# Decoder layer on one core: the first weight piece and the first part of x loaded as two halves each, the first products ordered block by block, new issue orders

## The chip, the cores and the metric

One core of a Trainium2 chip runs the whole kernel. TensorE (PE) multiplies, with its weight loads shown apart (PEld); VectorE (DVE), ScalarE (ACT) and GpSimd (POOL) work elementwise; SyncE (SP) issues most of the loads. The metric is the device time of one execution, in microseconds (us).

## What is computed

One layer of a decoder over 256 positions of 1024 channels, in float32: a normalised x times a wide input matrix, two attention mixers on parts of the product, two gates, an output projection with a residual, and an MLP.

```python
h = _rmsnorm(x, norm1_g[i])
proj = h @ w_in[i]                      # 1024 x 6308, split into q, k, v, gates
y_a = _nsa_mixer(q_a, k_c, v_c, k_s, v_s, k_w, v_w, g_nsa, ...)
y_b = _dilated_mixer(q_b, k_b, v_b)
mixed = sigmoid(g_ma) * (y_a @ w_o_a[i]) + sigmoid(g_mb) * (y_b @ w_o_b[i])
x = x + mixed @ w_out[i]
h2 = _rmsnorm(x, norm2_g[i])
x = x + square(relu(h2 @ w_up[i])) @ w_down[i]
```

## The kernel before

**Products in three parts.** Every float32 operand is split into a rounded high part and the rest: `wh` and `wl` of a weight piece, `hT[0]` and `hT[1]` of the scaled x. A product is the sum of `wh`·`hT[0]`, `wh`·`hT[1]` and `wl`·`hT[0]`. So a weight piece (128 partitions x 768 numbers, 384 KB; those of kv_w 840 numbers) takes three steps before PE can use all of it: its load into `raw`, ACT's rounding into `wh` (line 345; for the very first piece two casts on DVE, line 349), and DVE's subtraction into `wl` (line 350). A piece of an input projection then gives PE 12 matmuls (two row blocks `kk` of the piece, two halves `t` of the positions, three parts).

**The head.** x comes in four parts `xg[0..3]` of two blocks of 128 channels each; `xg[0]` begins with the 16 gains. `scale_x(k)` makes block k of `hT[0]` on ACT (line 415) and of `hT[1]` on DVE (line 416). `setup()` squares the four parts on ACT (`sx`, line 426), adds them on POOL (line 428), sums over partitions on PE (line 432), and gets the reciprocal root `rs` from DVE (`ss`, line 435) and POOL (line 436); POOL also makes the tables `ropeg` from `rope` and `gr` (lines 444 and 447). Before all that PE multiplies the tile `ones` by itself ten times (line 408). The first projections are the chunks kv_c (compressed keys and values, line 468), kv_s and kv_w (lines 479 to 481), then q_a and so on, with attention in between; the last stage is the MLP.

**What sets the order.** `ORDER` is a table of numbers for each engine: the instructions in the order in which the code writes them, renumbered into the order in which they are to be issued (`issue_order`). An engine issues strictly in that order, so an instruction that waits holds everything behind it on its engine; loads on SP and ACT hold the queue in the same way. Eight semaphores (DMAHW0 to DMAHW7 in the rows below) serve all loads in turn: a load that reuses one waits until its last user has landed.

**Buffers.** `once` gives a tile a place of its own. The tile `y` collects the attention outputs, `x1` holds x for the residual (line 1116) and the later sums.

Of the kernel before, what the change touches and what calls it, by code (L numbers as in the profile page):

```python
# [11 lines left out]
F32 = mybir.dt.float32  # L12
# [11 lines left out]
NT = 2  # L24
# [96 lines left out]
1 0 2 4 3 9+2 104 15 13 12 16 11 19 14 20 18 5 17 6 8 7 21+83 105+60 166 165 167+4 172 171 173+5 179 178  # L121
180+4 185 184 186+4 191 190 192+5 198 197 199+2""",
    "ACT": """
# [15 lines left out]
474 473 475+3 479 478 481 480 482 484 483 485+3 489 488 491 490 492 494 493 495+3 499 498 501 500 502+38""",  # L139
    "DVE": """  # L140
# [20 lines left out]
635+2 634 637+4 643 641 644 642 645+4 650+2 649 652+2""",  # L161
    "PE": """
# [83 lines left out]
def hybrid_layer(ctx: ExitStack, tc: tile.TileContext, A, out):  # L246
# [60 lines left out]
    def load_to(end):  # L307
        while len(raws) < min(end, len(pieces)):
# [4 lines left out]
            if q < 4:  # L313
                nc.sync.dma_start(xg[q], A["xg"][:, q * 512 + 16 * (q > 0):(q + 1) * 512 + 16])
# [972 lines left out]
```

## Time and profile before

| | |
|---|---|
| median of 3 runs | 459.05 us (459.05 to 459.7) |
| the profiled execution: time | 458.8 us |
| its span, first to last instruction | 457.0 us (1.8 us lie around it) |
| first product of the layer on PE | 11.12 us |
| mean granted TensorE clock | 0.993 of full speed |
| PE, PEld, DVE, ACT, POOL busy | 445.6, 431.1, 358.0, 284.2, 83.7 us |

Busy time is an average over stages with different limits: the head up to about 30 us, the attention stage up to about 260 us, and the rest. A row of the trace gives a start, a duration, the engine, the line, output<-inputs and shapes, and, where the engine stood idle before it, in brackets how long and what ended that.

### The profile page before, as it was taken

To read this page: it belongs to the slowest core of one execution; us is meant where nothing else is said; L and a number is where in the kernel's file an instruction comes from. 1 tells how busy PE (TensorE), PEld (TensorE's weight loads), DVE (VectorE), ACT (ScalarE), POOL (GpSimd) and SP (SyncE) were. 2 spreads that over 40 slices of the span, in tenths; PEclk is the share of its full clock that TensorE was granted. 3 is DMA by queue.
4 is the path that set the end of the run, shared out by engine and by line. 5 is a ranking of instruction groups with operands and counts; after the bars stand their busy time and mean duration, and the time that the engine had idled before them with its cause. 6 is when DMAs were issued, how large, how long until landed. Compare 5 with 4: busy or idle time off the path is not lost.

```text
span 457.0 us, 9071 instructions
## 1 busy us (share of the span) xinstructions
PE 445.6 (98%) x3413; PEld 431.1 (94%) x3413; DVE 358.0 (78%) x654; ACT 284.2 (62%) x622; POOL 83.7 (18%) x92
## 2 busy tenths in 40 slices
PE   4999999999999999999999999999999999999996
PEld 4999899899999999898999999999999999999996
DVE  3989999999999998899999886886856654555440
ACT  4855677678999778876775555665665634433330
POOL 2712121313041000200000001796322300000000
PEclk9799999999999999999999999999999999999999
DMA  8974586725535522541521647666666667677620
GB/s 304 367 244 146 154 287 181 236 89 167 157 105 141 171 70 71 175 140 68 162 82 42 199 128 231 201 193 186 205 184 195 183 187 210 185 216 199 179 78 13
DMA packets 29484, 76.92 MB, mean 168 GB/s; under 512 B 3664, under 2 KB 5120, under 8 KB 29312
## 3 DMA queue, kind: packets, MB, share of 16 engines
q1 hardware_dynamic: 28864, 74.77, 54.7%
q10 hardware_dynamic: 576, 1.57, 1.0%
q8 instruction: 27, 0.44, 0.4%
q14 instruction: 17, 0.14, 0.1%
HBM read 75.28 MB, written 1.05 MB: 167 GB/s over the span
## 4 chain that ended last, share of the span: by engine, by line
PE 93%; DVE 2%; ACT 2%; DMA 2%; issue 0%; ACTq 0%
PE acc L983 19%; PE acc L985 19%; PE acc L984 19%; PE acc L480 6%; PE acc L481 6%; PE acc L479 6%; PE tp L709 3%; PE acc L468 2%; DMA raw<-in_kv_c 2%; PE sp L754 1%; PE pvo L721 1%; ACT wh L345 1%; PE pvo L723 1%; PE tp L552 1%; PE dsp L920 1%; PE hacc L615 1%
## 5 line engine op out<-in xcount | busy, mean ns | idle before, releaser
L350 DVE TENSOR_TENSOR wl<-raw,wh 128x768 fp32r<-128x768 f32 (+2 forms) x183 | 177.6, 979 | 61.7 <-ACT wh L345 57.2
L345 ACT CAST wh<-raw 128x768 fp32r<-128x768 f32 (+1 forms) x182 | 149.6, 833 | 102.1 <-PE acc L984 74.5
L983 PE MATMUL acc<-u,wh 128*128 128x256 f32 x256 | 71.6, 280 | 0.0
L984 PE MATMUL acc<-u,wh 128*128 128x256 f32 x256 | 71.6, 280 | 0.0
L985 PE MATMUL acc<-u,wl 128*128 128x256 f32 x256 | 71.5, 279 | 0.0
L984 PE MATMUL acc<-h,wh 128*128 128x256 f32 x256 | 69.0, 280 | 0.0
L983 PE MATMUL acc<-h,wh 128*128 128x256 f32 x256 | 69.0, 279 | 0.0
L985 PE MATMUL acc<-h,wl 128*128 128x256 f32 x256 | 66.1, 279 | 0.0
L480 PE MATMUL acc<-wl,hT 128*128 128x384 f32 (+1 forms) x164 | 55.1, 350 | 0.3 <-DVE wl L350 0.3
L479 PE MATMUL acc<-wh,hT 128*128 128x384 f32 (+1 forms) x164 | 54.7, 348 | 0.0
L481 PE MATMUL acc<-wh,hT 128*128 128x384 f32 (+1 forms) x164 | 54.6, 347 | 0.0
L1159 POOL TENSOR_TENSOR r<-r 128x256 f32<-128x256 f32 x32 | 27.7, 866 | 128.7 <-ACT r L1158 127.5
L985 PEld LDWEIGHTS acc<-u,wl 128*128 128x128 f32 x256 | 48.2, 188 | 0.0
L983 PEld LDWEIGHTS acc<-u,wh 128*128 128x128 f32 x256 | 48.1, 188 | 0.0
L984 PEld LDWEIGHTS acc<-u,wh 128*128 128x128 f32 x256 | 48.1, 188 | 0.0
L983 PEld LDWEIGHTS acc<-h,wh 128*128 128x128 f32 x256 | 47.6, 188 | 0.0
L984 PEld LDWEIGHTS acc<-h,wh 128*128 128x128 f32 x256 | 47.4, 188 | 0.0
L985 PEld LDWEIGHTS acc<-h,wl 128*128 128x128 f32 x256 | 45.8, 188 | 0.0
L502 POOL TENSOR_TENSOR st<-st,nhalf 128x6 f32<-128x6 f32 (+1 forms) x16 | 21.6, 1348 | 92.8 <-DVE st L501 65.7
L984 PE MATMUL acc<-hT,wh 128*128 128x256 f32 x128 | 36.1, 293 | 0.0
L985 PE MATMUL acc<-hT,wl 128*128 128x256 f32 x128 | 35.9, 293 | 0.0
L983 PE MATMUL acc<-hT,wh 128*128 128x256 f32 x128 | 35.1, 290 | 0.0
(212 smaller groups left out, 986.9 us busy)
## 6 DMA issues: line engine op xcount, KB each, us to landing
raw<-in_cells SPq DMA_DIRECT2D x128, 384.0 KB, 3.4
raw<-in_cw SPq DMA_DIRECT2D x10, 384.0 KB, 3.2
raw<-in_q_a SPq DMA_DIRECT2D x8, 384.0 KB, 3.8
raw<-in_q_b SPq DMA_DIRECT2D x8, 384.0 KB, 3.4
raw<-in_k_b SPq DMA_DIRECT2D x8, 384.0 KB, 3.2
raw<-in_v_b SPq DMA_DIRECT2D x8, 384.0 KB, 3.1
raw<-in_kv_w SPq DMA_DIRECT2D x4, 420.0 KB, 6.7
raw<-in_kv_c ACTq DMA_DIRECT2D x4, 384.0 KB, 7.0
```

Source lines behind the costliest of these rows:

```text
L345: nc.scalar.copy(hi[:, :m], src)
L350: nc.vector.tensor_sub(lo[:, :m], src, f(hi[:, :m]))
L468: nc.tensor.matmul(acc[t][:, :n], hT[h][:, k, t * 128:(t + 1) * 128], w[:, kk * n:(kk + 1) * n], start=h == 0 and k == 0 and w is hi, stop ...
L479: nc.tensor.matmul(o, hT[0][:, k, ts], hi[:, c], start=k == 0, stop=False)
L480: nc.tensor.matmul(o, hT[0][:, k, ts], lo[:, c], start=False, stop=False)
L481: nc.tensor.matmul(o, hT[1][:, k, ts], hi[:, c], start=False, stop=k == 7)
L502: nc.gpsimd.tensor_tensor(st[:, 1, :h], st[:, 0, :h], nhalf[:, :h], op=OP.pow)
L709: nc.tensor.transpose(pt[0:rows, i * 128:(i + 1) * 128], s, ident)
L983: nc.tensor.matmul(o, hi, a[0][k], start=start, stop=False)
L984: nc.tensor.matmul(o, hi, a[1][k], start=False, stop=False)
L985: nc.tensor.matmul(o, lo, a[0][k], start=False, stop=stop)
L1159: mul = nc.gpsimd.tensor_mul(r, r, r)
```

## The change

The first piece of kv_c is loaded as two halves of 384 columns (192 KB each), and `xg[0]` as 272 and 256 columns (136 and 128 KB), each half with a semaphore of its own. The matmuls of the first three pieces are written block by block. `y` and `x1` now ask for one shared place by a common tag. All five tables of `ORDER` are new; of these the diff shows a line each.

```diff
     "SP": """
-1 0 2 4 3 9+2 104 15 13 12 16 11 19 14 20 18 5 17 6 8 7 21+83 105+60 166 165 167+4 172 171 173+5 179 178
+0+4 12 10 14 4 17 20 16 5 21 13 9 15 11 18+2 6+3 22+80 105 102+3 106+60 167 166 168+4 173 172 174+5 180 179
...
     "ACT": """
-0+4 6 10 13 9 4+2 7+2 11 16 15 14 17 12 19+2 25+4 18 21 47 22 24 35 48 36 23 49 38 41 37 58 42 29+2 32+2 43
+0+7 10 9 8 11 7 16+2 12 14+2 26 20+2 13 27+2 18 29 25 24 19 22+2 33 36 48 34 37 30+2 39 49+2 59 32 55 51+3
...
             raw = raw_p.tile([128, n], F32, name="raw", tag="raw" if n <= PIECE else "rawg")
+            if q == 0:
+
+                nc.sync.dma_start(xg[0][:, 0:272], A["xg"][:, 0:272])
+                nc.scalar.dma_start(raw[:, 0:n // 2], src[:, 0:n // 2])
+                nc.sync.dma_start(xg[0][:, 272:528], A["xg"][:, 272:528])
+                nc.scalar.dma_start(raw[:, n // 2:n], src[:, n // 2:n])
+                raws.append(raw)
+                continue
             if q < 4:
-                nc.sync.dma_start(xg[q], A["xg"][:, q * 512 + 16 * (q > 0):(q + 1) * 512 + 16])
+                nc.sync.dma_start(xg[q], A["xg"][:, q * 512 + 16:(q + 1) * 512 + 16])
...
-                for h, w in ((0, hi), (1, hi), (0, lo)):
-                    for kk in range(2):
-                        k = i * 2 + kk
-                        for t in range(NT):
...
+                for h, w, kk in [(0, hi, 0), (0, hi, 1), (1, hi, 0), (1, hi, 1), (0, lo, 0), (0, lo, 1)]:
+                    k = i * 2 + kk
+                    for t in range(NT):
...
-    st_["y"] = once([128, 8, S], F32, "y")
+    st_["y"] = big.pool.tile([128, 8, S], F32, name="y", tag="y", bufs=1)
...
-    x1 = big.tile([128, 8, S], F32, name="x1", tag="y", bufs=1)
+    x1 = big.pool.tile([128, 8, S], F32, name="x1", tag="y", bufs=1)
```

The start of ACT's queue before: the four loads of kv_c, the load of the function table, and then two roundings of weight pieces (`wh`) and two squarings (`sx`) ahead of the first block of `hT`.

```order
L315 DMA raw_80<-in_kv_c 128x768
L315 DMA raw_83<-in_kv_c 128x768
L315 DMA raw_86<-in_kv_c 128x768
L315 DMA raw_89<-in_kv_c 128x768
L345 ACT_TABLE_LOAD
L345 CAST wh_160<-raw_83 128x768 [waits DMAHW3_49]
L426 ACTIVATE sx1_181<-xg1_77 128x512 [waits DMAHW1_49]
L345 CAST wh_215<-raw_86 128x768 [waits DMAHW5_49]
L426 ACTIVATE sx0_180<-xg0_76 128x512 [waits DMAHW2_49]
L415 ACTIVATE hT0_137<-xg0_76 128x256 x2
```

The same place after the change.

```order
L308 DMA raw_80<-in_kv_c 128x384
L310 DMA raw_80<-in_kv_c 128x384
L315 DMA raw_85<-in_kv_c 128x768
L315 DMA raw_88<-in_kv_c 128x768
L315 DMA raw_91<-in_kv_c 128x768 [waits DMAHW1_49]
L415 ACT_TABLE_LOAD
L415 ACTIVATE hT0_139<-xg0_76 128x256
L415 ACTIVATE hT0_139<-xg0_76 128x256 [waits DMAHW2_49]
L426 ACTIVATE sx0_182<-xg0_76 128x512
L415 ACTIVATE hT0_139<-xg1_77,xg0_76 128x256 [waits DMAHW4_49]
L415 ACTIVATE hT0_139<-xg1_77,xg0_76 128x256
L426 ACTIVATE sx1_183<-xg1_77 128x512
```

`hT` moved to the front, and each block waits for its own part of x. There are five loads now, and the fifth reuses the semaphore of the first half of `xg[0]` (DMAHW1), so the table load and all behind it stand behind that landing.

The start of DVE's queue before: the two casts of the first piece, three subtractions (`wl`), then `hT[1]`.

```order
L349 CAST wh_155<-raw_80 128x384 [waits DMAHW0_49]
L349 CAST wh_155<-raw_80 128x384
L350 TENSOR_TENSOR wl_156<-raw_80,wh_155 128x768 [waits DVE_49]
L350 TENSOR_TENSOR wl_161<-raw_83,wh_160 128x768 [waits DMAHW3_49,Activation_49]
L350 TENSOR_TENSOR wl_216<-raw_86,wh_215 128x768 [waits DMAHW5_49,Activation_49]
L416 SCALAR_TENSOR_TENSOR hT1_138<-xg0_76,hT0_137 128x256 [waits DMAHW2_49,Activation_49]
```

The same place after the change.

```order
L416 SCALAR_TENSOR_TENSOR hT1_140<-xg0_76,hT0_139 128x256 [waits DMAHW1_49,Activation_49]
L349 CAST wh_157<-raw_80 128x384 [waits DMAHW0_49]
L416 SCALAR_TENSOR_TENSOR hT1_140<-xg0_76,hT0_139 128x256 [waits DMAHW2_49,Activation_49]
L349 CAST wh_157<-raw_80 128x384 [waits DMAHW3_49]
L350 TENSOR_TENSOR wl_158<-raw_80,wh_157 128x768 [waits DVE_49]
L416 SCALAR_TENSOR_TENSOR hT1_140<-xg1_77,xg0_76,hT0_139 128x256 [waits DMAHW4_49,Activation_49]
```

The two blocks of `hT[1]` now stand ahead of the two casts, so DVE's first instruction waits for ACT's first block of `hT[0]`, and the first cast stands behind it.

ACT's queue before, about 20 us later, at the first reading of `rs` (POOL makes `rs`; `vSW` and `y` are products times `rs`; `wh_243`, `wh_265` and `wh_269` are the second to fourth piece of kv_s).

```order
L345 CAST wh_326<-raw_273 128x840 [waits DMAHW3_49]
L345 CAST wh_243<-raw_94 128x768 [waits DMAHW5_49,DVE_49,PE_49]
L345 CAST wh_265<-raw_96 128x768 [waits DMAHW7_49,DVE_49,PE_49]
L562 ACTIVATE vSW_295<-acc_462,rs_140 128x3x64 [waits PE_49,Pool_49]
L345 CAST wh_269<-raw_98 128x768 [waits DMAHW1_49]
L573 ACTIVATE y_291<-acc_150,rs_140 128x384 [waits DVE_49,PE_49,Activation_49]
```

The same place after the change; those three pieces are now `wh_245`, `wh_267` and `wh_271`.

```order
L345 CAST wh_328<-raw_275 128x840 [waits DMAHW1_49,DVE_49]
L572 ACTIVATE y_293<-acc_152,rs_142 128x384 [waits PE_49,Pool_49]
L572 ACTIVATE y_285<-acc_151,rs_142 128x384 [waits PE_49]
L345 CAST wh_245<-raw_96 128x768 [waits DMAHW0_49]
L345 CAST wh_267<-raw_98 128x768 [waits DMAHW1_49]
L345 CAST wh_271<-raw_100 128x768 [waits DMAHW2_49,DVE_49]
```

The two `y`, which wait for `rs` (Pool_49), moved ahead of all three of these pieces.

On SP the load of `gr` moves from the 7th to the 17th place and waits for the second piece of kv_w; the load of `x1` moves from the 8th to the 103rd place, into the attention stage. On POOL `rs` moves ahead of four of the six tables, behind the two first ones, and the tile `ones` is set before `vC` and one of the two `pc`.

## Rows read from the trace of the kernel before

**Rows 1.** Two windows: busy us (instructions) of PE, PEld, DVE, ACT, POOL; clock; DMA.

```profile
12.00:260.00 248.00, 247.02 (x1747) 233.04 (x1746) 235.63 (x495) 182.62 (x455) 37.31 (x33) 0.99 0.51 155
260.00:457.00 197.00, 193.14 (x1648) 192.88 (x1646) 118.03 (x154) 96.24 (x160) 43.11 (x47) 1.00 0.61 176
```

**Rows 2.** PE's longest wait of the span: total us, times, longest.

```profile
PE acc L468 <- ACT hT L415: 4.1, 1, 4.1
```

**Rows 3.** Timeline of PE: the warm-up, the first product, two spacings, the 38th product.

```profile
2.45 4.58 PE L408 MATMUL acc<-ones 128*128 128x128 f32 x20 [2.45 <-POOL ones L403]
11.12 3.13 PE L468 MATMUL acc<-wh,hT 128*128 128x384 f32 x8 [4.09 <-ACT hT L415]
...
15.01 0.52 PE L468 MATMUL acc<-wh,hT 128*128 128x384 f32 x1
15.33 0.52 PE L468 MATMUL acc<-wl,hT 128*128 128x384 f32 x1
...
17.53 0.51 PE L468 MATMUL acc<-wh,hT 128*128 128x384 f32 x2
17.88 0.51 PE L468 MATMUL acc<-wl,hT 128*128 128x384 f32 x2
...
22.04 0.42 PE L468 MATMUL acc<-wh,hT 128*128 128x384 f32 x1
```

**Rows 4.** Windows of the head: columns as in rows 1; the last are clock, DMA share, GB/s.

```profile
0.00:5.00 5.00, 2.55 (x12) 2.56 (x13) 0.00 (x0) 1.28 (x1) 1.86 (x11) 1.00 0.62 185
10.00:11.00 1.00, 0.00 (x0) 0.00 (x0) 0.83 (x1) 1.00 (x4) 0.26 (x1) 0.63 1.06 417
11.00:12.00 1.00, 0.88 (x3) 0.89 (x4) 1.00 (x2) 1.00 (x4) 1.00 (x1) 0.50 1.04 398
17.00:18.00 1.00, 1.00 (x7) 1.00 (x6) 1.00 (x2) 0.15 (x1) 0.17 (x1) 0.96 1.09 403
```

**Rows 5.** Timeline of ACT and its queue in the head.

```profile
0.72 2.10 ACTq L315 DMA_DIRECT2D raw<-in_kv_c  x4
2.85 1.28 ACT L345 ACT_TABLE_LOAD   x1 [2.85 <-issue]
10.57 0.89 ACT L415 ACTIVATE hT<-xg 128x256 fp32r<-128x256 f32 x2
```

**Rows 6.** Timeline of DVE in the head.

```profile
5.01 0.63 DVE L349 CAST wh<-raw 128x384 fp32r<-128x384 f32 x2 [5.01 <-DMA raw<-in_kv_c]
8.39 0.96 DVE L350 TENSOR_TENSOR wl<-raw,wh 128x768 fp32r<-128x768 f32 x1 [1.75 <-ACT wh L345]
10.16 0.96 DVE L350 TENSOR_TENSOR wl<-raw,wh 128x768 fp32r<-128x768 f32 x1 [0.82 <-ACT wh L345]
11.10 1.84 DVE L416 SCALAR_TENSOR_TENSOR hT<-xg,hT 128x256 fp32r<-128x256 f32 x2
15.55 0.47 DVE L416 SCALAR_TENSOR_TENSOR hT<-xg,xg,hT 128x256 fp32r<-128x256 f32 x1
23.70 3.10 DVE L350 TENSOR_TENSOR wl<-raw,wh 128x840 fp32r<-128x840 f32 x3
29.87 1.93 DVE L350 TENSOR_TENSOR wl<-raw,wh 128x768 fp32r<-128x768 f32 x2 [1.23 <-PE acc L480]
```

**Rows 7.** Timeline of POOL in the head.

```profile
10.74 1.52 POOL L428 TENSOR_TENSOR sx<-sx,sx 128x512 f32<-128x512 f32 x1 [3.58 <-ACT sx L426]
18.44 5.24 POOL L444 TENSOR_TENSOR ropeg<-rope,gr 128x256 f32<-128x256 f32 x5 [1.26 <-DMA rope<-in_rope]
23.63 0.72 POOL L436 TENSOR_TENSOR rs<-ss,nhalf 128x2 f32<-128x2 f32 x1
```

**Rows 8.** DMA issues: KB each, median us from issue to landing.

```profile
x<-in_xg SPq DMA_DIRECT2D x1, 1024.0 KB, 8.9
gr<-in_gr SPq DMA_DIRECT2D x1, 384.0 KB, 6.9
```

**Rows 9.** DVE's longest wait for PE from 10 to 260 us: total us, times, longest.

```profile
DVE nm L791 <- PE sp L756: 2.1, 5, 0.6
```

More of the change, by code (lines that the diff above doesn't have):

```diff
@@ L120 @@
     "SP": """
-1 0 2 4 3 9+2 104 15 13 12 16 11 19 14 20 18 5 17 6 8 7 21+83 105+60 166 165 167+4 172 171 173+5 179 178
-180+4 185 184 186+4 191 190 192+5 198 197 199+2""",
+0+4 12 10 14 4 17 20 16 5 21 13 9 15 11 18+2 6+3 22+80 105 102+3 106+60 167 166 168+4 173 172 174+5 180 179
+181+4 186 185 187+4 192 191 193+5 199 198 200+2""",
     "ACT": """
[15 rows of a table removed]
-474 473 475+3 479 478 481 480 482 484 483 485+3 489 488 491 490 492 494 493 495+3 499 498 501 500 502+38""",
-    "DVE": """
[20 rows of a table removed]
-635+2 634 637+4 643 641 644 642 645+4 650+2 649 652+2""",
-    "PE": """
[60 rows of a table removed]
-2575+17 2597 2592+3 2598 2595 2599+20 2620 2619 2621+767""",
[15 rows of a table added]
+474 476+3 480 479 482 481 483 485 484 486+3 490 489 492 491 493 495 494 496+3 500 499 502 501 503+38""",
+    "DVE": """
[20 rows of a table added]
+649 652+2""",
+    "PE": """
[52 rows of a table added]
+2139+2 2163+2 2129+10 2141+6 2188+2 2147+16 2212+2 2165+18 2187 2183+4 2190+22 2214+1174""",
     "POOL": """
-28 25 2 15 14 0+2 7 3+3 11+2 10 9 8 6 13 18 17 16 19+3 23+2 22 26+2 34+2 38 37 40 29 39 30 33 31 36 32 42 41
-45+5 44 50+5 56 55 57+4 62 61 63+11 43 74+14""",
+0 28 15 14 1+2 25 7 3+3 13 11 6 12 8 10 9 18+2 16+2 20+2 23 22 24 26+2 34+2 38+2 29 37 30 40 33 36 31+2 42
+41 45+3 43 50 48+2 51+2 44 53+2 56 55 57 59 58 60+28""",
 }
@@ L462, in proj @@
             if first and i < D["hh"]:
-                for h, w in ((0, hi), (1, hi), (0, lo)):
-                    for kk in range(2):
-                        k = i * 2 + kk
-                        for t in range(NT):
-                            nc.tensor.matmul(acc[t][:, :n], hT[h][:, k, t * 128:(t + 1) * 128],
-                                             w[:, kk * n:(kk + 1) * n], start=h == 0 and k == 0 and w is hi, stop=False)
+                for h, w, kk in [(0, hi, 0), (0, hi, 1), (1, hi, 0), (1, hi, 1), (0, lo, 0), (0, lo, 1)]:
+                    k = i * 2 + kk
+                    for t in range(NT):
+                        nc.tensor.matmul(acc[t][:, :n], hT[h][:, k, t * 128:(t + 1) * 128],
+                                         w[:, kk * n:(kk + 1) * n], start=h == 0 and k == 0 and w is hi, stop=False)
                 pe(12 * n / 2400)
```

180 rows, old and new, of the table ORDER are left out of this document.

## The prediction, made before the changed kernel ran

> **What bounds the kernel now.** I read the windows first, stage by stage. From 260 us to the end DVE works 118 of 197 us, while PE and its weight loads fill 193 [rows 1]: the last 197 us are PE's alone, the change leaves their work as it is, and whatever happens earlier shifts them. From 12 to 260 us both are nearly full: PE shows 247 of 248 us, but its weight loads only 233; DVE is busy 235.6, so it pauses 12.4 us in all [rows 1]. In this stretch neither can be moved far without the other. DVE makes every `wl`, and PE can't finish a weight piece without it.
>
> PE's waits come next: one is far longer than all others, 4.1 us for ACT's first `hT` [rows 2]. The timeline of the head shows why. The warm-up multiplications run from 2.45 to 7.03, and the first product starts at 11.12 [rows 3]. `hT` began on ACT at 10.57 [rows 5], although the first weight piece had landed at 5.01 [rows 6]. ACT was given other work first. The pause has a second price: the granted clock falls in the slice from 10 to 11 (0.63 in the mean, so at about 10.3), stays at 0.50, the lower of the two levels (1.2 GHz), and is back at 17 to 18 [rows 4]. In that stretch two products start 0.32 us apart, afterwards two take 0.35 together, 0.175 each [rows 3]. By 22.04 PE has started its 38th product of the layer [rows 3].
>
> **Head: when can the first product start?** In the first 5 us the DMA moves 185 GB/s x 5 us = 925 KB [rows 4], and the first piece of 384 KB lands at their end, since the other loads move beside it. The two first halves are 192 + 136 = 328 KB. The trace has no landing of such a half. Upper bound: no earlier than the whole piece, 5.0. Lower bound: the same end with only the missing half piece taken off at the 400 GB/s that the DMA reaches once it is full [rows 4], twice because two queues share it: 2 x 192 / 400 = 1.0, so 4.0. I take 4.2, nearer the lower end, because both queues now hold half as much ahead of it.
>
> ACT then has a wait that it did not have: the fifth load of its queue waits for the half of `xg[0]`, and the table load of 1.28 us stands behind it; before, it ran at 2.85 while nothing was there to work on [rows 5]. So: landing 4.2, one issue 0.4 (four took 2.10, so 0.5 at most), table load 1.28, makes 5.9; first block of `hT[0]` 0.45 (two took 0.89), 6.35. DVE's first block of `hT[1]`, which now stands ahead of the cast, 0.47 when POOL is idle [rows 6], 6.8; the cast 0.31, 7.1; with three hand-overs of about 0.1 each (10.57 + 0.45 to 11.12 is 0.1) **the first product starts at 7.4**, 3.7 earlier. From the bounds it is 7.2 to 8.7, the upper with 0.5 for the issue and 0.92 for `hT[1]` as at 11.10 [rows 6].
>
> The table load is where the Trainium skill and the trace differ. "ScalarE: Activation LUTs", section "What ACT_TABLE_LOAD costs", counts about 2.66 us for a load with its drain. By that figure the first product would start 1.4 later, at 8.8, and the sum below would lose as much; the 1.28 of [rows 5] is used.
>
> **Clock.** `ones` is set earlier (one `pc` and `vC` go behind it), so the warm-up ends by about 6.2, my estimate from the sum of those two fills, 0.8. The pause before the first product is then about 1.2 us instead of 4.1, and before the change the clock still stood at full for about 3.3 us after the last warm-up (7.03 to 10.3). So I expect 1.00 all through the head. That returns half of the 5.9 us from 11.12 to 17.0, 2.95.
>
> **PE by the 38th product.** 38 x 0.175 = 6.65 from 7.4 makes 14.05; waits for `hT[1]` and `wl`, which DVE delivers one by one (0.92 a block beside POOL's additions of 1.52 each [rows 6, 7]), I put at 1.3: three pieces, each with about 0.4. So 15.3 instead of 22.0: **PE gains 6.7**.
>
> **DVE by about 30 us.** Its work up to there is the same instructions in another order. It begins at 6.4 instead of 5.01: -1.4. Its three pauses (1.75 and 0.82 for ACT, 1.23 for PE [rows 6]) go: +3.8. Against that stands a new wait: after the ninth `wl` DVE needs the second kv_s piece, `wh_245`, which on ACT stands behind both `y`, which need `rs`. By my walk DVE gets to `ss` at about 21.5; `gr`, now the 17th load, is issued at about 13.9 (behind the landing of the second kv_w piece, issued near 7) and lands 6.9 later at most [rows 8], 20.8; two tables of 1.05 each (5.24 / 5) and `rs` 0.72 [rows 7] make 22 to 23.6; two `y` and a rounding add 1.5. DVE's three `wl` at this place began at 23.70 before, the third at about 25.4 [rows 6]; `wl_246` would begin between 23.5 and 25. The wait costs 0 to 2.4. Part of it is free, because POOL's tables slow DVE only when DVE works. I take 0.4: **DVE gains 2.0** (0 to 2.4).
>
> **The sum.** From 30 to 260 us the gain lies between DVE's 2.0 and PE's 6.7. DVE is the fuller engine, so I start from 2.0. Of its remaining 11.2 us of pauses (12.4 less the 1.23) some are waits for PE, 2.1 in the largest group [rows 9], and these shrink with PE ahead; I put that at 1.3. The sum is 3.3.
>
> The other edits are put at nothing. The load of `x1`, 1024 KB, leaves the head, where it took 8.9 us to land and about 2.5 us of a full DMA [rows 4, 8]; that helps the later weight pieces, and is part of their being in time above. At its new place, late in the attention stage, the DMA is half idle (0.51 busy from 12 to 260 [rows 1]); if it came too late for the residual, each us would be lost whole. The block order moves matmuls without adding any. The new order of the attention stage I can't price from the trace; its bounds are DVE's 11.2 us of pauses as a gain and the same again as a loss, and I see no reason for a sign, so it stands in the range.
>
> 458.8 - 3.3 = 455.5 for an execution like the profiled one. That one lies 0.25 under the median of 459.05, so the predicted time is **455.7 us**.
>
> **Rivals.** *PE's gain carries through*: DVE's pauses later are mostly waits for products, and its lead in buffered pieces lets it give way. Time: 459.05 - 6.7 = 452.3. For it: DVE waits for PE at 28.6 with all buffers full [rows 6]. Against it: 95% busy.
>
> *The halves land no earlier.* The Trainium skill's "DMA: Bandwidth & Descriptors", section "Bandwidth", asks for loads batched to 1 MiB or more, which speaks against cutting 384 KB in two. As a mechanism here: both halves land at 5.0, as the whole did; the first product starts at 8.2, and the gain shrinks by 0.8 to 2.5, 456.5. Against it: with 925 KB moved by 5.0, the wait was mostly for other loads' bytes.
>
> *No change*: the head's gain is spent where DVE is full; the wait for `rs` costs its whole 2.4, and the new attention order adds DVE pauses of about 2. Time: 459.
>
> *Slower*: `gr` lands late. In the head SP's loads stood in line for up to 8.9 us [rows 8], and now ropeg, `rs`, both `y`, three kv_s pieces and all that DVE splits from them stand behind this one load. Each us after 20.8 delays DVE by one; from 25 (20.8 + 3.3 + the 0.9 by which `ss` is later than needed) it is slower than before. A landing at 27 gives 461. Against it: `x1` has left that line.
>
> **Chances and range.** Forecast 0.47, PE's gain whole 0.2, halves no earlier 0.1, no change 0.13, slower 0.1. A change under 0.2%, 0.9 us, can't be told from none in this kernel. Faster: 0.47 + 0.2 + 0.1, with 0.01 from the fourth case: 0.78; same 0.11; slower 0.11. The range for 8 in 10 reaches from a little beyond the second case, 451.5, to the fourth, 459.2; the forecast's own is 453.5 to 457.5.
>
> **What would show it.** First product at 7.2 to 8.7; the table load right before the first `hT`, at about 4.6 instead of 2.85; clock 1.00 in every slice of the head; the 38th product near 15.3; DVE without the pauses of 1.75, 0.82 and 1.23, but with one before the second kv_s piece; from 260 us on the same spacing of products. I am wrong if the clock falls all the same (2 to 3 us less), if `rs` comes after 24, or if the attention stage's pauses change by more than 3 us.

## The result: slower, and both losses lie behind the head

The changed kernel takes 464.7 us (463.62 to 465.88, four runs) against 459.05: ratio 1.0121, 95% interval 1.0094 to 1.0147. Its profiled execution took 464.48 us with a span of 462.7. The prediction was 455.7, so it missed the sign. I split the run at PE's first product of `mT` (the mixed attention output), which is the 1645th of 3388 matmuls in both kernels with the same work ahead of it and behind it.

| us | before | after |
|---|---|---|
| first product of the layer | 11.12 | 7.03 |
| first product of `mT` | 248.32 | 247.07 |
| from there to the last product | 204.54 | 211.43 |
| of this, the last 768 products (input `u`) | 89.85 | 90.57 |

The head did what it was meant to do, and 1.25 us of it are left at 247 us. Behind that, 6.9 us are lost. Columns are those of [rows 1]; here are the two stretches of after, the second to 463:

```profile
12.00:260.00 248.00, 246.06 (x1733) 228.61 (x1736) 232.88 (x489) 180.23 (x451) 36.75 (x32) 1.00 0.52 156
260.00:463.00 203.00, 195.23 (x1639) 194.73 (x1637) 119.85 (x157) 96.45 (x161) 44.21 (x47) 0.99 0.60 171
```

PE is busy 195.2 us in a stretch that before filled with 193.1 [rows 1], and in the new stretch there are 7.8 us without PE, before 3.9. So PE waits more and also works longer. Where it waits is the first line of PE's waits, and the timeline of PE around it:

```profile
PE tp L1166 <- POOL sqs L1126: 3.5, 1, 3.5
PE acc L467 <- ACT sx L426: 1.4, 1, 1.4
```

```profile
310.96 0.28 PE L982 MATMUL acc<-h,wh 128*128 128x256 f32 x1
311.08 0.28 PE L983 MATMUL acc<-h,wh 128*128 128x256 f32 x1
314.91 0.71 PE L1166 MATMUL tp<-sqs,ones 128*128 128x256 f32 x2 [3.55 <-POOL sqs L1126]
...
316.48 0.41 PE L982 MATMUL acc<-h,wh 128*128 128x256 f32 x1
316.69 0.41 PE L983 MATMUL acc<-h,wh 128*128 128x256 f32 x1
```

In the MLP, PE sums `sqs` (squares of the new x, added up by POOL, for the second norm) over the partitions. PE stops 3.55 us for POOL's last addition, and the products behind it start 0.21 us apart instead of 0.12. The windows tell why: the granted clock goes to 0.50, the lower level, and is back between 318 and 320.

```profile
312.00:314.00 2.00, 0.00 (x0) 0.00 (x0) 1.06 (x2) 0.64 (x4) 1.94 (x3) 1.00 0.48 174
314.00:316.00 2.00, 1.09 (x5) 1.04 (x6) 1.67 (x2) 0.81 (x2) 1.98 (x2) 0.87 0.61 186
316.00:318.00 2.00, 2.00 (x12) 2.00 (x11) 1.39 (x3) 0.72 (x2) 1.17 (x2) 0.50 0.57 155
318.00:320.00 2.00, 2.00 (x15) 2.00 (x15) 1.39 (x3) 1.14 (x2) 0.37 (x1) 0.78 0.63 159
```

Before, the same matmul started at 316.75 without a wait, and POOL's last addition ended at 311.89, a margin of 4.86:

```profile
316.75 0.59 PE L1167 MATMUL tp<-sqs,ones 128*128 128x256 f32 x2
311.04 0.85 POOL L1127 TENSOR_TENSOR sqs<-sqs 128x256 f32<-128x256 f32 x1
```

The timeline of POOL after shows the addition ending at 314.85, 2.96 later, behind two waits for ACT in the first MLP blocks:

```profile
284.20 1.23 POOL L1158 TENSOR_TENSOR r<-r 128x256 f32<-128x256 f32 x1 [3.75 <-ACT r L1157]
290.95 3.62 POOL L1158 TENSOR_TENSOR r<-r 128x256 f32<-128x256 f32 x3 [3.24 <-ACT r L1157]
...
314.02 0.83 POOL L1126 TENSOR_TENSOR sqs<-sqs 128x256 f32<-128x256 f32 x1
```

PE's table for the MLP differs too: the matmul, instruction 2187, now stands 40 products earlier. 40 products of 0.12 are about 4.7 us of margin taken; 3.0 more are taken by the later squares, and about 0.7 by PE's own lead at this place. So 4.86 of margin became a wait.

That is one loss. The other is no wait at all: PE works without a gap from 340 to 400 us in both kernels, and still does less. First before, then after:

```profile
340.00:400.00 60.00, 60.00 (x515) 60.00 (x514) 34.42 (x45) 30.13 (x49) 7.25 (x9) 1.00 0.68 191
```

```profile
340.00:400.00 60.00, 60.00 (x511) 60.00 (x510) 33.73 (x43) 30.73 (x51) 9.51 (x11) 1.00 0.69 190
```

515 products became 511 at the same clock; over the last 768 the spacing is 90.57 / 768 = 0.1179 instead of 0.1170.

**The head after**, from the timelines of ACT, DVE, PE and POOL, which answer to [rows 3, 5, 6, 7]:

```profile
1.65 2.60 ACTq L315 DMA_DIRECT2D raw<-in_kv_c  x3
4.29 1.28 ACT L415 ACT_TABLE_LOAD   x1 [4.29 <-DMA xg<-in_xg]
5.58 0.91 ACT L415 ACTIVATE hT<-xg 128x256 fp32r<-128x256 f32 x2
```

```profile
6.12 0.49 DVE L416 SCALAR_TENSOR_TENSOR hT<-xg,hT 128x256 fp32r<-128x256 f32 x1 [6.12 <-ACT hT L415]
...
25.20 2.49 DVE L350 TENSOR_TENSOR wl<-raw,wh 128x768 fp32r<-128x768 f32 x2 [0.36 <-ACT wh L345]
```

```profile
7.03 1.96 PE L467 MATMUL acc<-wh,hT 128*128 128x384 f32 x8 [1.36 <-ACT sx L426]
...
15.25 0.52 PE L478 MATMUL acc<-wh,hT 128*128 128x420 f32 x2
```

```profile
3.95 0.19 POOL L440 COPY g<-xg 128x8 f32<-128x8 f32 x1 [1.54 <-DMA xg<-in_xg]
22.65 0.72 POOL L436 TENSOR_TENSOR rs<-ss,nhalf 128x2 f32<-128x2 f32 x1 [2.85 <-DVE ss L435]
```

The first half of x was there at 3.95. The table load waited for it as foreseen, at 4.29; the first product came at 7.03 and the 38th at 15.25. In before the 38th product that reads `hT` is at 20.95; the row at 22.04 that [rows 3] shows for it is the 43rd:

```profile
20.95 0.35 PE L480 MATMUL acc<-wl,hT 128*128 128x420 f32 x1
```

The pause ahead of the first product is 1.36, and the products behind it run at the full clock: eight take 1.96, where [rows 3] has 3.13 for eight.

### The profile page after: what moved, and what is told of

The parts are those of the page before. It is cut to its first block, busy times and chain, and to the rows that moved or that the text cites. A ratio compares the mean times of both kernels' runs of the same rounds, so it can differ in the third digit from the quotient of the medians.

```text
span 462.7 us, 9075 instructions
## 1 busy us (share of the span) xinstructions
PE 449.8 (97%) x3410; PEld 431.0 (93%) x3413; DVE 357.8 (77%) x654; ACT 283.5 (61%) x622; POOL 84.8 (18%) x92
## 4 chain that ended last, share of the span: by engine, by line
PE 85%; POOL 5%; DMA 4%; DVE 3%; issue 2%; ACT 1%; SPq 0%; POOLq 0%; ACTq 0%
PE acc L982 18%; PE acc L984 18%; PE acc L983 18%; PE acc L479 5%; PE acc L478 5%; PE acc L480 5%; PE tp L708 3%; POOL r L1158 2%; POOL sqs L1126 1%; PE sp L753 1%; DMA xg<-in_xg 1%; PE dsp L919 1%; POOL sqs L1125 1%; DMA raw<-in_kv_w 1%; DVE wl L350 1%
## 5 line engine op out<-in xcount | busy, mean ns | idle before, releaser
L350 DVE TENSOR_TENSOR wl<-raw,wh 128x768 fp32r<-128x768 f32 (+2 forms) x183 | 180.0, 997 | 60.2 <-ACT wh L345 57.7
L984 PE MATMUL acc<-h,wl 128*128 128x256 f32 x256 | 71.1, 284 | 0.0
L982 PE MATMUL acc<-h,wh 128*128 128x256 f32 x256 | 71.1, 283 | 0.0
L983 PE MATMUL acc<-h,wh 128*128 128x256 f32 x256 | 70.9, 283 | 0.0
L1158 POOL TENSOR_TENSOR r<-r 128x256 f32<-128x256 f32 x32 | 31.5, 988 | 132.7 <-ACT r L1157 132.7
L982 PEld LDWEIGHTS acc<-h,wh 128*128 128x128 f32 x256 | 48.5, 191 | 0.1
L984 PEld LDWEIGHTS acc<-h,wl 128*128 128x128 f32 x256 | 48.5, 191 | 0.0
L983 PEld LDWEIGHTS acc<-h,wh 128*128 128x128 f32 x256 | 48.4, 191 | 0.0
L501 POOL TENSOR_TENSOR st<-st,nhalf 128x6 f32<-128x6 f32 (+1 forms) x16 | 23.7, 1479 | 98.7 <-DVE st L500 91.0
```

Of the source, the lines that this page charges most:

```text
L350: nc.vector.tensor_sub(lo[:, :m], src, f(hi[:, :m]))
L501: nc.gpsimd.tensor_tensor(st[:, 1, :h], st[:, 0, :h], nhalf[:, :h], op=OP.pow)
L982: nc.tensor.matmul(o, hi, a[0][k], start=start, stop=False)
L983: nc.tensor.matmul(o, hi, a[1][k], start=False, stop=False)
L984: nc.tensor.matmul(o, lo, a[0][k], start=False, stop=stop)
L1158: mul = nc.gpsimd.tensor_mul(r, r, r)
```

## The experiments

Theories: **1**, PE's table asks for the sum of squares too early (**1a**: because POOL's table makes the squares late); **2**, the new order of the attention stage costs what the head gains; **3**, the order of the last stage slows the products. When these left the spacing over, a fourth came up: the place of the weight buffers in on-chip memory. A ratio is to the kernel before, run on the same chip, with its 95% interval; before's own median was 459.05 to 459.72 on these chips, so differences of a few tenths between medians of different chips are read by the ratios.

### The sum of squares

**a_pe_late**: after, with the matmul where before has it (DVE's two instructions that go with it moved alike).

```diff
 PE:  ... 2212+2
-2165+18 2187 2183+4 2190+22 2214+1174
+2165+22 2190+22 2214+14 2187 2228+1160
```

> The changed kernel with one matmul moved: the one that sums the eight squares stands 40 matmuls later in PE's table, where it stood before the change (its two DVE operations move with it). Theory 1 (PE's table put this matmul too early, and the wait of 3.55 us there, with the low clock behind it, is the loss): the wait falls to 0.3 us or less, the clock stays 1.00 from 310 to 322 us, the first product on u starts about 5 us earlier (near 363), and the time is 459 to 460 us. Rival (the wait only covers another delay, such as late weight pieces or DVE splits): another wait of 3 us or more shows between 311 and 330 us, and the time stays at 463 to 465 us.

460.0 us, 1.0013 (1.0004 to 1.0022): 4.7 us of the 5.65 are back. The row of the wait is gone; PE's window from 300 to 320, first of after, then of this run, shows no pause and a full clock:

```profile
300.00:320.00 20.00, 16.45 (x125) 16.20 (x125) 16.57 (x18) 9.39 (x19) 17.16 (x17) 0.91 0.65 186
```

```profile
300.00:320.00 20.00, 20.00 (x171) 19.95 (x170) 16.06 (x17) 9.60 (x21) 17.61 (x17) 1.00 0.65 179
```

46 products more in the same 20 us. The head gained less here: the pause before the first product was 1.68, and the clock fell behind it; behind after's 1.36 it did not.

```profile
7.00:8.00 1.00, 0.68 (x3) 0.42 (x4) 0.96 (x4) 1.00 (x4) 0.00 (x0) 1.00 1.04 390
8.00:9.00 1.00, 1.00 (x4) 1.00 (x5) 1.00 (x2) 1.00 (x3) 0.37 (x1) 0.53 1.04 403
```

**b_pool_squares**: after, with POOL's second square and its addition ahead of two `r`.

```diff
-41 45+3 43 50 48+2 51+2 44
+41 45+5 43 50+3 44
```

> The changed kernel with POOL's second square and its addition put back ahead of two r products, as before the change; PE's table as changed. Theory 1a (POOL's order made the squares 3 us late, and that alone makes PE wait): the last square is added near 312 instead of 314.9, PE's wait falls from 3.55 to about 0.7 us, the clock stays 1.00, and the time is 459.5 to 460.5 us. Theory 1b (PE's place alone is at fault, POOL works without a pause up to the end of the squares either way): the wait stays over 2.5 us and the time at 463 to 465 us.

466.48 us, 1.0145 (1.0127 to 1.0163): slower, the wait is 4.0, and the low clock behind it lasts twice as long, from 314.5 to 321.3. POOL now waits 1.49 for ACT's `r` where it did not in after, and its last addition starts at 315.53 instead of 314.02. Theory 1a fell: POOL's order by itself is not what makes the squares late.

**d_before_late**: before, with the matmul 40 products earlier and one square behind one more `r`.

```diff
 PE, before:
-2214+18
+2187 moved from behind 2214+14 to behind 2183+2
 POOL, before:
-45+5 44 50+5
+45+3 44 50 48+2 51+4
```

> The kernel before with only the two suspected moves of the late tables: PE's sum of squares 40 matmuls earlier, POOL's second square behind one r product more. Theory 1: it loses as the changed kernel did; PE waits 2.5 to 4 us for the squares near 312 us, the clock falls there, and the time is 462.5 to 465 us. Rival (that place costs nothing by itself): 459 to 460 us.

460.49 us, 1.0026 (1.0016 to 1.0036), with a wait of only 1.0 and no fall of the clock: before's squares, even with this one moved back, are ready so much earlier that the two moves cost 1.4 (1.2 by the ratio). The full loss takes both, the early matmul and the squares as late as after's tables make them.

### Where in the run it is lost

Four kernels join the tables of the two: all five engines follow one order up to a point and the other behind it. In **c_head_only** after's order runs to DVE's 64th instruction, in **g_head_to_70** to its 120th (about 70 us), then before's. **i_late_tables_before** is after to PE's 1700th matmul, then before; **j_late_tables_after** is before to there, then after with the matmul late.

```diff
 each engine's table
-the order of after
+its first part, then what is left in the order of before   (c, g, i)
+the first part of before, then what is left in the order of after   (j)
```

> The changed kernel's code, loads and order up to the 64th DVE operation (about 45 us); from there every engine goes on in the order of the kernel before. Theory 1 (the head gains, the new order of the attention stage gives it back, the sum of squares loses the rest): the gain of about 3.5 us that DVE shows at 50 to 65 us is kept to a part or whole, no wait over 1 us in the last 190 us, time 455.5 to 458. Rival 2 (nothing gained in the head can be kept, since DVE is full from 45 to 260 us whatever the order): 458.5 to 459.5. Rival 3 (the split loads or the shared queue cost something later): over 460.

463.22 us, 1.0081 (1.0068 to 1.0094), with 204.54 from the first `mT` product, exactly before's. The seam made a wait of its own (5.3 us, `tp` for `vk`), so nothing can be said of the head from it.

> As c_head_only, with a later seam: the changed kernel's order up to the 120th DVE operation (about 70 us), where the two orders have nearly the same work behind them, then the order of the kernel before. No wait of 5 us at the seam this time (c_head_only's was at its seam, on vk). Theory 2 (the head's gain for DVE is about 1.3 us at 90 us, and the new attention order gives it back): 457.4 to 458.4. Rival (the attention order costs nothing, the head brings nothing in the end): 459.5 to 460.2, as a_pe_late.

456.83 us, 0.9949 (0.9937 to 0.9961), under both expectations: the first kernel that is faster. First `mT` product at 246.71, and 204.5 behind it.

> The changed kernel's order on every engine up to PE's 1700th matmul (about 255 us, through the whole attention stage), then the order of the kernel before. The first product on mT is PE's 1645th matmul in every kernel so far, so the time splits there: 247.1 us ahead of it and 211.4 behind it in the changed kernel, 248.3 and 204.5 before. Theory 3 (the attention order costs nothing, all of the loss lies in the last 200 us, in the order of the late tables): first mT near 247.1, 204.5 behind it, time 457.6 to 458.4. Rival (theory 2: the new attention order gives back the head's gain): first mT near 248.3 or later, time 459 to 460.

459.04 us, 0.9998 (0.9989 to 1.0007). The wait is gone, but the last 768 products take 90.84, under before's own tables. Theory 3 fell.

> The kernel before up to PE's 1700th matmul, then the changed kernel's order, with the sum of squares at its old place as in a_pe_late. Theory 3: the late tables alone cost 1.5 us or more, through a spacing of products of 0.118 us or more instead of 0.1173; 206.0 to 207 us behind the first mT instead of 204.5, time 460.5 to 461.5. Rival (the spacing belongs to something in the head or in the attention stage, such as the load of x1 or the split loads): 204.5 behind the first mT, time 459.0 to 459.6.

459.1 us, 1.0005 (0.9996 to 1.0014), the last 768 in 89.78, under after's tables. The spacing follows what was done before 248 us, not the order of the products themselves.

### The place of the weights

In the built kernels one thing went with the spacing: an address. With the attention order of after, one more buffer of 4224 bytes a partition lies ahead of the mask than in g, and most weight tiles (327 of 366) start at 480 bytes past a multiple of 512, where in before (320) and g (323) they start at 352. c, d and j have 352 too; a, b, e, f, h and i have 480. A longer mask tile, of which nothing more is used, moves what lies behind it and no instruction. `u`, the other operand of the last 768 products, lies ahead of the mask, at the same places in all twenty kernels, so that of these products only the weights are moved:

```diff
-    mask = const.tile([128, MASK_COLS], BF16, name="mask")
-    nc.sync.dma_start(mask, A["mask"])
+    mask = const.tile([128, MASK_COLS + 64], BF16, name="mask")
+    nc.sync.dma_start(mask[:, :MASK_COLS], A["mask"])
```

+64 columns are 128 bytes (n, o, q); p has +80. m has +336, and there the mask itself is placed elsewhere too.

**m_weights_352**: a, with the weights back at 352.

> The kernel of a_pe_late with one edit: the mask's buffer is 672 bytes a partition longer (unused), so that the weight buffers behind it lie at addresses of 352 modulo 512 bytes a partition, as in the kernel before, and not at 480. No instruction is added or moved. Theory 4 (the last 1.5 us of loss come from where the weights lie in the on-chip memory): the 768 products on u take 89.8 us instead of 90.57, 204.5 to 204.9 us lie behind the first mT instead of 206.08, time 458.0 to 458.9. Rival (the address only goes along with the attention order, and something else in that order sets the spacing): 90.5 and 206 as in a_pe_late, time 459.6 to 460.4.

457.62 us, 0.9964 (0.9951 to 0.9976), 2.4 less than a; the last 768 in 90.33, only a third of the way to 89.85. 1.4 of the gain lies ahead of `mT` (246.19 against 247.60), and the clock fell in the head here too (pause 1.6).

**n_before_weights_480**: before, with the weights at 480.

> The kernel before with the mask's buffer 128 bytes a partition longer, so that the weight buffers lie at 480 modulo 512 instead of 352; nothing else. Theory 4: the 768 products on u take 90.5 to 91.1 us instead of 89.85, 206 to 207 us behind the first mT instead of 204.5, time 460.3 to 461.3. Rival: 89.85, 204.5 and 458.9 to 459.4 us.

461.98 us, 1.0063 (1.005 to 1.0076): 2.9 more than before, 91.05 for the last 768, with nothing else changed.

**o_weights_96**: a, with the weights at 96.

> The kernel of a_pe_late with the mask's buffer 128 bytes longer, weights at 96 modulo 512. If what counts is the address modulo 256 (352 and 96 are alike), it goes as m_weights_352: 89.8 us for the products on u, time 458.0 to 458.9. If it is modulo 512 or more, or the rival of theory 4 holds: 90.5 or another value, time 459.6 to 460.4.

456.85 us, 0.9951 (0.9936 to 0.9966), 3.15 less than a: first `mT` product at 246.35, 204.52 behind it, 89.64 for the last 768. The windows of 340 to 400 of n and of o:

```profile
340.00:400.00 60.00, 60.00 (x510) 60.00 (x509) 33.21 (x44) 29.49 (x48) 7.88 (x10) 1.00 0.69 193
```

```profile
340.00:400.00 60.00, 60.00 (x516) 60.00 (x515) 34.13 (x45) 29.17 (x46) 7.64 (x9) 1.00 0.71 198
```

Before's order slows to 510 with the address, and after's order reaches 516. Theory 2 fell with it: o runs after's attention order and is at `mT` 1.97 ahead of before. (It is 0.36 ahead of g, which has before's order, but g's seam made a wait of 1.3 for `vq`.)

**q_changed_weights_96**: after, with the weights at 96 and nothing else.

> The changed kernel itself with only the mask's buffer 128 bytes a partition longer (weights at 96 modulo 512); PE's sum of squares stays at its early place. If the two losses add (4.7 us for the sum of squares, 2.4 to 3.1 for the weights' address): the wait for the squares and the low clock behind it stay, time 461.3 to 462.3. Rival (the wait swallows what the address gives, since the squares' end does not move with PE): 463 to 464.7.

462.32 us, 1.0066 (1.0053 to 1.0078); the wait for `sqs` remains at 3.68, the last 768 take 89.64. The two losses add, within the noise.

### The head by itself

**e_pe_delay**: a, with 21 warm-up multiplications instead of 10. **f_table_early**: a, with ACT's fifth load behind the first two `hT`, so that the table load waits for nothing. **h_whole_loads**: a, with the first piece and `xg[0]` each loaded whole.

```diff
 e
-"warm": 10
+"warm": 21
 f, ACT
-0+7 10 9 8
+0+4 5+2 4 10 9 8
 h
-four loads of halves
+nc.sync.dma_start(xg[0], A["xg"][:, 0:528])
+nc.scalar.dma_start(raw, src)
```

> The kernel of a_pe_late (the changed kernel with PE's sum of squares at its old place) with 21 warm-up multiplications instead of 10, so that PE is held up and starts its first product about 3 us later (near 10.1), with no pause and so at full clock; nothing else is moved. Theory 2 (up to 150 us DVE sets the pace, so that PE's lead in the head is worth nothing): the time stays within 0.8 us of a_pe_late's 460.0. Rival (PE's lead carries through, as the prediction's second rival had it): about 3 us more, 463.

459.93 us, 1.0018 (1.0009 to 1.0027): the first product starts at 8.27, 1.02 later than in a, and the time is a's. That does not show that PE's lead is worth nothing, though the expectation would have it so: in a the clock fell behind the first product, in e it did not, and so e's 38th product started earlier than a's, at 15.00 against 15.71. First a, then e:

```profile
7.25 2.78 PE L467 MATMUL acc<-wh,hT 128*128 128x384 f32 x8 [1.68 <-ACT sx L426]
8.27 1.66 PE L467 MATMUL acc<-wh,hT 128*128 128x384 f32 x8
```

e's first `mT` product is 0.83 earlier than a's (246.77), and its last 768 take 91.06 instead of 90.57. What becomes of PE's lead is read better from before and after: 5.7 us at the 38th product that reads `hT`, 3.4 at the 100th, 2.7 at the 300th (about 75 us), 1.25 at `mT`.

> The kernel of a_pe_late with ACT's fifth load moved behind the first two hT activations, so that the table load no longer stands behind that load's wait for the half of xg. The table load starts near 2.8 instead of 4.5, the first hT near 4.2 instead of 5.8, the first product near 5.8, DVE begins near 4.8 instead of 6.3. Theory 2 (DVE sets the pace): DVE's 1.4 us earlier start shows to 0.7 to 1.4 us in the time: 458.6 to 459.3. Rival (DVE then waits at the ninth wl for the late fourth piece or for rs): 459.8 to 460.5.

459.62 us, 1.0019 (1.0005 to 1.0033): the first product starts at 5.46, 1.8 earlier, and the first `mT` product at 246.30, 1.3 earlier than in a (in whose head the clock fell). Behind it 0.8 are lost again, with 91.01 for the last 768: the edit moved the weights too (345 tiles at 480, 327 in a). The time can't be told from a's; the runs lie between 458.95 and 461.55.

> The kernel of a_pe_late with the first weight piece and the first part of x each loaded whole, as before the change; everything else as changed. If the halves bring the head's gain: whole loads land at about 5.0, ACT's fifth load and the table load behind it wait as long, the first product starts near 8.4 instead of 7.25, and DVE begins 0.8 to 1.1 us later; time 460.5 to 461.2. Rival (the halves land no earlier): first product near 7.3, time 460.0 as a_pe_late.

460.6 us, 1.003 (1.0017 to 1.0043), but its first product comes at 6.52, before a's and before after's:

```profile
2.92 1.28 ACT L413 ACT_TABLE_LOAD   x1 [2.92 <-issue]
5.08 0.91 ACT L413 ACTIVATE hT<-xg 128x256 fp32r<-128x256 f32 x2 [0.88 <-DMA xg<-in_xg]
```

With whole loads `hT` starts at 5.08, with halves at 5.58: what the halves gain in landing, the fifth load's wait for one of them takes away again through the table load. h's larger time lies behind `mT`, with 92.04 for the last 768, so it says nothing of the halves; l does.

### The repairs put together

**k_table_early_70** is g with f's edit, **l_whole_70** g with h's, **p_best_weights_0** k with the weights at 0, **r_all_repairs** f with o's mask.

```diff
 k: g, and ACT  0+7 10 9 8  ->  0+4 5+2 4 10 9 8
 l: g, and the two whole loads of h
 p: k, and      MASK_COLS  ->  MASK_COLS + 80
 r: f, and      MASK_COLS  ->  MASK_COLS + 64
```

> The kernel of g_head_to_70 with ACT's fifth load behind the first two hT activations, as in f_table_early. If DVE's earlier start counts: first product near 5.5, first mT 0.4 to 0.8 us earlier than in g_head_to_70 (246.7), time 456.0 to 456.5. Rival (the gain ends at the wait for rs and at the seam): 456.6 to 457.0, as g_head_to_70.

455.88 us, 0.9929 (0.9915 to 0.9942), the fastest of all. Its profiled execution has 0.41 on g's at the first `mT` product (246.30) and 0.23 behind it, where the last 768 take 89.60 instead of 89.80: a part of its gain is the place of the weights again (336 tiles at 352, 323 in g).

> The kernel of g_head_to_70 with the first weight piece and the first part of x loaded whole. In h_whole_loads the whole loads let the first product start at 6.52, earlier than the halves' 7.0 to 7.25, since ACT's table load then waits for nothing, and what made that kernel slower came in the last 200 us. If that holds: first product near 6.5, first mT at 246.2 to 246.8, time 456.2 to 457.0. Rival (the halves do bring time): 457.4 or more.

456.51 us, 0.994 (0.9926 to 0.9954): 0.3 less than g. The halves bring nothing.

> The kernel of k_table_early_70 with the mask's buffer 160 bytes longer, weights at 0 modulo 512. Theory 4 says only that another residue can give another spacing: 89.0 to 92 us for the products on u (89.60 at 352), time 455.2 to 458. Rival (address without effect): 89.6 and 455.6 to 456.2.

460.84 us, 1.0036 (1.0023 to 1.0049): 5.0 more than k by the address alone. k, then p:

```profile
340.00:400.00 60.00, 60.00 (x517) 60.00 (x516) 34.18 (x44) 29.34 (x46) 7.09 (x9) 1.00 0.70 192
```

```profile
340.00:400.00 60.00, 60.00 (x503) 60.00 (x502) 33.47 (x44) 29.08 (x47) 7.22 (x9) 1.00 0.66 188
```

A start at a multiple of 512 gave the slowest products of all: 92.16 for the last 768, 89.60 in k.

> The changed kernel with all three repairs: sum of squares at its old place, weights at 96 modulo 512, ACT's fifth load behind the first two hT activations. o_weights_96 (the first two) had 456.85. If DVE's earlier start counts as in k_table_early_70 (about 0.9): 455.7 to 456.3, about as k_table_early_70's 455.88. Rival (it ends at the wait for rs): 456.6 to 457.0.

457.3 us, 0.9953 (0.9938 to 0.9967), level with o. Its first `mT` product is 0.6 earlier than o's, but the last 768 take 90.34 although the weights lie at 96, as in o. So the start past a multiple of 512 is not the whole rule.

## Why the prediction was wrong, step by step

**The step that failed** is the first: "the last 197 us are PE's alone, the change leaves their work as it is, and whatever happens earlier shifts them", with "the same spacing of products" from 260 us on. The bound was read rightly, the inference not. All five tables were new to their end, and I compared only their heads and the attention stage. Forty products of 0.12 us lay between PE's two places for one matmul, against a margin of 4.86 that two rows of before gave; with the squares 3 us later that is a wait of about 3, with PE's lead of 0.7 of 3.5, and 3.55 was measured. With the slow clock behind it, it cost 4.7 (after against a). Nor is equal work equal time: the spacing moved with the buffers' addresses, which the order decides through the allocation. That is 3.15 (a against o); n shows 2.9 for it on before's own order.

**The sum as the runs give it**: 459.05, less 2.2 for the head (o, which has neither loss), plus 3.15, plus 4.7, is 464.7. By the ratios the terms are 2.25, 2.85 and 4.96. They are differences along one chain, so that they add up is no test. q, n and d stand outside it: q, with the first loss alone, should be at 459.05 - 2.2 + 4.7 = 461.55, ratio 1.0054 (1.0059 by the ratios), and measured 1.0066.

**First product** at 7.4 (7.2 to 8.7): 7.03, a little under the range. The landing at 4.2 was 3.95; the table load stood where foreseen, at 4.29 for 4.6. The 1.28 of [rows 5] held again, and there is no second pause behind it: `hT` starts at 5.58, 0.01 after its end. The 2.66 us that the Trainium skill gives for a load with its drain ("ScalarE: Activation LUTs", "What ACT_TABLE_LOAD costs") is not seen in this place.

**Clock in the head** at 1.00: right for after's products, and by luck, since the length of the pause does not decide it. a and m fell at pauses of 1.68 and 1.6, k did not at one of 1.90, and in o, where the warm-ups had not yet brought the clock up, eight products took 2.92, the lower level, behind a pause of only 0.60. First o, then k, then o's window:

```profile
6.88 2.92 PE L467 MATMUL acc<-wh,hT 128*128 128x384 f32 x8 [0.60 <-ACT sx L426]
9.92 1.66 PE L475 MATMUL acc<-wh,hT 128*128 128x384 f32 x8 [1.90 <-ACT wh L353]
8.00:9.00 1.00, 1.00 (x5) 1.00 (x5) 1.00 (x3) 1.00 (x3) 0.00 (x0) 1.00 1.05 405
```

The window prints 1.00 for products that start 0.32 apart: in o the trace records no clock until 11.07, and a window shows 1.00 where nothing is recorded. So the 1.00 of the first 5 us in [rows 4] was no evidence either. The warm-ups there start 0.21 apart nearly to their end, after's last ones 0.11.

**PE by the 38th product** at 15.3: 15.25. **It gains 6.7**: 5.7, because the 22.04 that it was counted from is not the 38th product but the 43rd. Of these 5.7 only 1.25 are left at `mT` (1.97 in o), so the rival that "PE's gain carries through" is out.

**DVE's 2.0 and the 1.3 of later pauses**, 3.3 in all, measured 2.2 in time (o), 1.97 of it at `mT`: right in sign, over by half of what was measured. `rs` ended at 23.37, inside 22 to 23.6, and DVE's wait at the second kv_s piece was 0.36 for the 0.4 taken. So I put the difference down to the 1.3, the term with the least under it; no run separates it.

**The rivals.** "The halves land no earlier" was wrong as put, since the half was there at 3.95, but its consequence holds: g with halves is no faster than l without. "`gr` lands late" did not happen. "No change" through attention pauses did not either: o, with after's attention order, reaches `mT` 1.97 ahead of before. The late load of `x1` made no wait for PE. None of the rivals was what happened; the slower side came from a place that I had closed.

**What stays open**: why the squares end 3 us later, and by what rule an address sets the spacing. The first is narrowed to the late tables: from the first `mT` product to the end of the squares it is 63.6 us in before and 63.4 in i, which has before's late tables, but 67.8 in after and 67.7 in j, which has after's. In after POOL stood idle for `r` for 8.1 us in the first MLP blocks, where before has 4.9. Which engine's table does it was not tried, but POOL's alone does not (b), nor does the early matmul (a, which has it late, ends the squares at 315.4). For the second, the tiles into which the weights are loaded (`raw`) and the output tiles are moved with the weights by every pad; a pad on the weight buffers alone was not tried.

## What to carry to other kernels

When a table of orders is new, compare it to its end on the engine that sets the time: for each of its instructions that waits for another engine, take the margin in the old trace and subtract the places by which it moved, times the spacing. When a stretch has the same products, no gap and full clock but fewer of them in 60 us, look at where the operands lie in memory before looking for a wait, and test it with a pad that moves no instruction. Before a load is cut in two, see what queues behind its landing: here the function table did, and the halves brought nothing (g against l). Moving that issue back brought the first product 1.8 us forward (f against a), and about 0.4 us of that were seen at `mT` where the clock fell in neither (k against g); whether halves help then was not tried.

## What the runs showed of the hardware

- **Matmul spacing depends on buffer addresses.** Over the last 768 products, whose other operand `u` never moved, the same instructions at a full clock took 89.60 (k) or 92.16 us (p), 0.1167 or 0.1200 each, after a shift of 160 bytes; 160 bytes were worth 5.0 us of 456. Weights at 352 gave 89.60 to 90.33, 480 gave 90.57 to 91.06 and in h 92.04, 96 gave 89.64 twice and 90.34 once, 0 gave 92.16.
- **The length of a pause does not tell whether the clock falls.** In the head it stayed at the full level through 1.36 (after), 1.5 (q) and 1.90 us (k), and was at 0.50 to 0.53 behind 1.6 (m) and 1.68 (a). In the MLP, waits of 3.55 (after) and 4.0 (b) were followed by some 3 to 4 and 7 us at 0.50, in which products start 0.21 apart instead of 0.12.
- **A window's 1.00 can mean that nothing was recorded.** In o the windows print 1.00 from the start, but until about 11 us products start 0.32 apart, as at 0.50 in before [rows 3], and 0.175 behind that.
